# A five-part edit of a fused two-block kernel: transposes a step later, keys copied by DMA, held weights, ordered tables, split low parts

## The chip, the cores and the metric

The kernel runs on one core of a Trainium2 chip. The metric is the device time of one execution in microseconds; the time given for a kernel is the median of its runs. Profiles come from one further execution, recorded by the hardware profiler.

## The reference, cut to what matters

Input x is 512 tokens by 1024 channels, float32. A first block has three sublayers, each with an RMS norm before and after and a residual: a mixer (pooled channels, sparse attention over the best 128 keys, gates), cross attention to 256 memory rows (4 heads of 128), and a SwiGLU feed-forward of width 2816. Then two hybrid layers follow, the part that most of the change touches:

```python
proj = einsum("bld,de->ble", x, w_in)
q, k, v, z_attn, z_ssm, xbc, dt_raw = split(proj)
attn = sliding_window_attention(q, k, v, sinks) * silu(z_attn)   # 16 heads of 64, 4 key heads, window 128
xbc = silu(causal_depthwise_conv(xbc, conv_w, conv_b))
y = ssd_chunked(xs, dt, a, bm, cm) + xs * d_skip
ssm = gated_rmsnorm(y, z_ssm, ssm_norm_w)                        # two groups of 512 channels
x = layer_norm(ALPHA * x + concat(attn, ssm) @ w_out, ln_g, ln_b)
```

## The kernel before, in words

**Tiling.** Channels lie on the 128 partitions and tokens along the free axis, so an activation is eight tiles of 128 x 512, and token halves A and B are columns 0 to 255 and 256 to 511. A projection is made in units of 128 output channels. float32 precision is kept by splitting each operand into a high part in the fast format fp32r and a low part, the remainder: a unit is 24 matmuls (high x high, high x low for eight channel tiles in `mm3`, L147 and L148, then low x high, L152).

**Weights.** `weights` (L100) loads 512 KB into one of three `wraw` tiles by SyncE's queue, ScalarE casts it into one of three `whi` tiles (L107), VectorE writes the remainder into one of three `wlo` tiles (L108). `held` (L111) does the same into tiles of the large pools G or R (34 tiles each), in pieces of 512 columns, so that the three small pools stay free. `units_by_k` (L160) runs four units at once, channel tile by channel tile; the three weights in it that come from `weights` are all in use until its end.

**Order.** Only SyncE's instructions keep the order of the program text. On the other engines a planner at compile time orders instructions by their place in the text, by its own costs and by when it expects operands, and gives out tiles; `issue_after` adds an edge that keeps one instruction behind another on its engine.

**Norms.** `chain`, made by `post_norm` or by a hybrid layer, is a generator: `begin` starts it inside the next layer's first unit, `pump` takes it further by steps, so that the norm of half B runs beside the next layer's units on half A. `inv_sqrt` (L211) needs ScalarE's Ln and Exp, and preloads the table set that has both when a tanh has run since; L224 puts that preload behind the last square.

**The places of the change.** The mixer's first three units (L462 to L472) run by channel tile, with a step of the pending norm after each. The memory layer (L724) takes the output weights of its eight output units from `wo`, of which the first pair is held in G and the others come from `weights`; each of four weight tiles serves two units, first for half A and then for B. The feed-forward (L822) then asks for its first three weights and holds a fourth. A hybrid layer runs gate units, the convolutions and the state-space part, then the keys (L1108; each half of 64 rows is copied to the other 64 partitions by GpSimd at L1114), the values' projection, the second group's norm and the attention loop (L1213). A step of that loop has the scores and the softmax of one head (`scores`: four matmul pairs, VectorE's sum and maximum, ScalarE's Exp, then the scaling by VectorE and GpSimd at L1169), the transposes of the head before (`transposed`: seven, L1183, copied out by ScalarE at L1186), a unit (the next queries or a gate) and, every second step, `values` (L1198) for a pair of heads. GpSimd makes the slopes' table of each head at L1142 in one of nine tiles that the softmax rows share.

Of the kernel before, what the change touches and what calls it, by code (L numbers as in the profile page):

```python
# [14 lines left out]
S = 512  # L15
# [46 lines left out]
class Kern:  # L62
# [37 lines left out]
    def weights(self, src, n=1024):  # L100
# [6 lines left out]
        nc.scalar.copy(hi[:, :n], raw[:, :n])  # L107
        nc.vector.tensor_tensor(lo[:, :n], raw[:, :n], hi[:, :n].bitcast(F32), ALU.subtract)  # L108
        return hi, lo
# [97 lines left out]
    def tanh(self, out, src, scale=1.0):  # L207
        self.ln_set = False
        self.nc.scalar.activation(out, src, AF.Tanh, scale=scale)  # L209

    def inv_sqrt(self, rs, src, u, eps=None, scale=1.0):  # L211
# [7 lines left out]
        if self.ln_set:  # L219
            nc.scalar.activation(rs, src, AF.Ln, **kw)  # L220
        else:
            self.ln_set = True
            with self.tc.issue_after(self.last_sq.ins):
                nc.scalar.preload_act_table_set("natural_log_exp_and_others")  # L224
            with self.tc.issue_after(nc.cur_bb.bb.instructions[-1]):
                nc.scalar.activation(rs, src, AF.Ln, **kw)
# [228 lines left out]
    def mixer(self):  # L455
# [8 lines left out]
        for c in self.HALVES:  # L464
            for k, (x, y) in enumerate(h):
                for pt, m, (whi, wlo) in first:
                    o, cc = pt[:m, c], slice(k * m, k * m + m)
                    nc.tensor.matmul(o, whi[:, cc], x[:, c], start=k == 0, stop=False)
                    nc.tensor.matmul(o, whi[:, cc], y[:, c], start=False, stop=False)
                    nc.tensor.matmul(o, wlo[:, cc], x[:, c], start=False, stop=k == 7)  # L470
                self.pump(1)
            self.pump()  # L472
# [251 lines left out]
    def memory(self):  # L724
# [77 lines left out]
        queries(B, lambda k: values(k // 2, A, pa[k // 2]) if k % 2 else None)  # L802
        wo += [self.weights(a["w_o_mem"][1]), self.weights(a["w_o_mem"][2])]
        for j in range(8):
            if j == 4:
                wo.append(self.weights(a["w_o_mem"][3]))
            out(j, A)
            if j < 4:
                pb.append(logits(j, B))
        for j in range(4):  # L810
            values(j, B, pb[j])
            if j == 0:
                self.head = chain(A)
                self.begin()
        for j in range(8):
            self.pump(1)
            out(j, B)
        self.pump()
        self.head = chain(B)


    def ffn(self):  # L822
# [21 lines left out]
        g = [self.f("ht") for _ in range(2)]  # L844
        first = [self.weights(z) for z in (a["w_gate"][0], a["w_up"][0], a["w_gate"][1])]
        first.append(self.held(a["w_up"][1], "R"))
        for c in self.HALVES:
# [39 lines left out]
    def hybrid(self, L):  # L887
# [220 lines left out]
        for j in range(2):  # L1108
            pt = self.proj(W[j], h)
            ks = [[self.r("G") for _ in range(2)] for _ in range(2)]  # L1110
            for (kh, kl), r, o in zip(ks, (top, bot), (bot, top)):
                self.split(pt[r], kh[r], kl[r], 0.125)
                for t in (kh, kl):
                    nc.gpsimd.tensor_copy(t[o], t[r].bitcast(F32))  # L1114
            kt.append(ks)
# [96 lines left out]
        prs = None  # L1212
        for t in range(17):  # L1213
            j, e_ = divmod(t, 2)
            nxt = scores(t, q) if t < 16 else None
            if t:
                pts[t - 1] = transposed(prs)
            if e_ == 1:
                pz = self.proj(W[32 + j], h)
                g = gate[j] = self.f("R")  # L1220
                self.tanh(g, pz, scale=0.5)
                nc.vector.scalar_tensor_tensor(g, g, 1.0, pz, ALU.add, ALU.mult)
                if j < 7:
                    q = qn
            elif j < 7:
                qn = queries(j + 1)
            if e_ == 0 and t:
                i = j - 1
                pos = values(i, (pts[2 * i], pts[2 * i + 1]))
                nc.vector.tensor_tensor(gate[i], gate[i], pos, ALU.mult)  # L1230
                cat[i] = self.pair(gate[i], "R", 0.5)
            prs = nxt
# [190 lines left out]
```

## Time and profile before

| | |
|---|---|
| median of 3 runs | 1671.53 us (1671.07 to 1672.05) |
| the profiled execution | 1672.5 us, its span 1670.7 us |
| TensorE (PE) busy | 1621.6 us, 97% |
| VectorE (DVE) | 1115.1 us, 67% |
| ScalarE (ACT) | 838.0 us, 50% |
| GpSimd (POOL) | 239.2 us, 14% |
| mean granted TensorE clock | 0.993 |

Times in rows are microseconds from the start of the span unless marked ns; L147 is line 147. In a line of a wait, the instruction on the left waited for the one on the right. In a timeline's line, the figure in brackets is the idle time of the engine before the instruction and what ended it. PEld is TensorE's weight load, which runs beside its matmuls. Roughly, the mixer lies at 39 to 400 us, the memory layer at 380 to 463, the feed-forward at 463 to 820, the hybrid layers at 840 to 1250 and 1255 to 1671; their attention loops are at 1025 to 1154 and 1436 to 1565.

### The profile page before, as it was taken

The numbers are of one execution on the slowest core, as the hardware profiler recorded it, in microseconds if no ns is written. First come the engines' busy times: TensorE is split into PE (matmuls) and PEld (weight loads), VectorE is DVE, ScalarE is ACT, GpSimd is POOL, SyncE is SP. The second block draws the span as 40 slices with busy tenths as digits, with TensorE's granted clock in tenths as the row PEclk, the third lists the DMA queues.
The fourth block names the chain that finished last, engine by engine and source line by source line (L and its number), as shares of the span: only waits on it lengthen the run. The fifth ranks groups of instructions, "written<-read, shape, count | busy, mean of one in ns | idle before, by whom it ended". The sixth has DMA issues, their size and how long they took to land.

```text
span 1670.7 us, 24187 instructions
## 1 busy us (share of the span) xinstructions
PE 1621.6 (97%) x9046; PEld 1362.4 (82%) x9046; DVE 1115.1 (67%) x2199; ACT 838.0 (50%) x1648; POOL 239.2 (14%) x267
## 2 busy tenths in 40 slices
PE   8999999999999999999999999999999999999996
PEld 5778888889888888889988677777998867777786
DVE  6779866548885545523677888765487788866447
ACT  4443255336763233223554776664355477766424
POOL 2010113010200000000000223221230023222121
PEclk9999999999999999999999999999999999999998
DMA  6522322143143233234632122111452211212133
GB/s 223 196 96 76 119 96 76 64 151 119 62 150 104 89 101 101 87 102 129 212 93 89 38 64 89 64 64 56 141 177 82 79 38 57 96 61 65 66 103 112
DMA packets 57719, 166.50 MB, mean 100 GB/s; under 512 B 6673, under 2 KB 15841, under 8 KB 57601
## 3 DMA queue, kind: packets, MB, share of 16 engines
q1 hardware_dynamic: 49216, 155.21, 29.0%
q10 hardware_dynamic: 8384, 9.73, 1.8%
q8 instruction: 71, 1.16, 0.3%
q14 instruction: 48, 0.39, 0.1%
HBM read 158.61 MB, written 8.93 MB: 100 GB/s over the span
## 4 chain that ended last, share of the span: by engine, by line
PE 78%; DVE 11%; ACT 5%; issue 2%; POOL 2%; DMA 1%; SPq 0%; ACTq 0%; DVEq 0%; POOLq 0%
PE psmm L148 21%; PE psmm L152 21%; PE psmm L147 21%; DVE wlo L108 2%; POOL w L1169 2%; PE psmm L175 2%; PE psmm L173 2%; PE psmm L174 2%; ACT w L1164 1%; DVE w L1160 1%; DVE G L130 1%; PE pstr L1061 1%; PE pstr L1183 1%; PE pslg L561 1%; PE pslg L1020 1%
## 5 line engine op out<-in xcount | busy, mean ns | idle before, releaser
L147 PE MATMUL psmm<-G,whi 128*128 128x512 f32 (+1 forms) x1196 | 468.5, 393 | 1.3 <-ACT whi L107 1.3
L148 PE MATMUL psmm<-G,whi 128*128 128x512 f32 (+1 forms) x1196 | 464.3, 389 | 0.0
L108 DVE TENSOR_TENSOR wlo<-wraw,whi 128x1024 fp32r<-128x1024 f32 (+3 forms) x265 | 320.4, 1210 | 184.8 <-ACT whi L107 99.2
L107 ACT CAST whi<-wraw 128x1024 fp32r<-128x1024 f32 (+3 forms) x265 | 270.9, 1025 | 340.3 <-PE psmm L148 291.3
L152 PE MATMUL psmm<-G,wlo 128*128 128x512 f32 (+1 forms) x1196 | 296.3, 388 | 0.0
L148 PEld LDWEIGHTS psmm<-G,whi 128*128 128x128 f32 x1196 | 225.3, 188 | 47.2 <-issue 4.2
L147 PEld LDWEIGHTS psmm<-G,whi 128*128 128x128 f32 x1196 | 225.3, 188 | 47.2 <-issue 2.4
L152 PEld LDWEIGHTS psmm<-G,wlo 128*128 128x128 f32 x1196 | 222.7, 189 | 46.4 <-issue 1.5
L148 PE MATMUL psmm<-R,whi 128*128 128x256 f32 (+1 forms) x732 | 222.7, 326 | 0.0
L147 PE MATMUL psmm<-R,whi 128*128 128x256 f32 (+1 forms) x732 | 222.6, 326 | 0.0
L147 PEld LDWEIGHTS psmm<-R,whi 128*128 128x128 f32 x732 | 139.2, 190 | 11.8 <-issue 0.3
L148 PEld LDWEIGHTS psmm<-R,whi 128*128 128x128 f32 x732 | 139.2, 190 | 11.5
L152 PE MATMUL psmm<-R,wlo 128*128 128x256 f32 (+1 forms) x732 | 138.1, 326 | 0.0
L152 PEld LDWEIGHTS psmm<-R,wlo 128*128 128x128 f32 x732 | 112.8, 190 | 11.5
L198 POOL TENSOR_TENSOR acc<-acc,sq 128x512 f32<-128x512 f32 (+1 forms) x42 | 53.4, 1272 | 454.4 <-ACT sq L197 454.4
L1164 ACT ACTIVATE w<-w,st 128x256 f32<-128x256 f32 (+1 forms) x128 | 60.2, 471 | 33.5 <-DVE st L1162 33.2
L1169 POOL TENSOR_SCALAR w<-w,st 128x256 f32<-128x256 f32 x64 | 46.1, 730 | 134.6 <-DVE st L1167 127.0
L209 ACT ACTIVATE sq<-ht 128x512 f32<-128x512 f32 (+1 forms) x48 | 29.4, 613 | 58.5 <-DVE ht L907 29.3
L1049 POOL TENSOR_TENSOR R<-R,R 128x512 f32<-128x512 f32 x16 | 21.7, 1353 | 228.3 <-ACT R L1048 228.3
L907 DVE SCALAR_TENSOR_TENSOR ht<-psmm,cwh,ht 128x511 f32<-128x511 f32 (+2 forms) x72 | 53.5, 743 | 1.2
L837 DVE TENSOR_TENSOR sq<-psmm,G 128x512 f32<-128x512 f32 (+1 forms) x24 | 15.5, 645 | 57.3 <-PE psmm L152 57.3
L566 POOL TENSOR_TENSOR G<-G,G 128x384 f32<-128x384 f32 (+2 forms) x24 | 28.9, 1217 | 162.1 <-DMA G<-ts 93.4
(348 smaller groups left out, 2701.8 us busy)
## 6 DMA issues: line engine op xcount, KB each, us to landing
wraw<-w_in SPq DMA_DIRECT2D x112, 512.0 KB, 3.4
wraw<-w_out SPq DMA_DIRECT2D x56, 512.0 KB, 3.8
wraw<-w_down SPq DMA_DIRECT2D x24, 512.0 KB, 3.5
wraw<-w_gate SPq DMA_DIRECT2D x22, 512.0 KB, 3.3
wraw<-w_up SPq DMA_DIRECT2D x22, 512.0 KB, 3.3
wraw<-w_down SPq DMA_DIRECT2D x12, 384.0 KB, 3.2
wraw<-w_proj_attn SPq DMA_DIRECT2D x8, 512.0 KB, 3.4
ts<-t SPq DMA_DIRECT2D x4, 640.0 KB, 7.0
```

What stands on the lines that cost most here:

```text
L107: nc.scalar.copy(hi[:, :n], raw[:, :n])
L108: nc.vector.tensor_tensor(lo[:, :n], raw[:, :n], hi[:, :n].bitcast(F32), ALU.subtract)
L147: nc.tensor.matmul(out, whi[:, c], xh, start=start and k == 0, stop=False)
L148: nc.tensor.matmul(out, whi[:, c], xl, start=False, stop=False)
L152: nc.tensor.matmul(out, wlo[:, c], xh, start=False, stop=stop and k == n - 1)
L173: nc.tensor.matmul(o, whi[:, cc], xh[:, c], start=k == 0 and i % 2 == 0, stop=False, skip_group_check=True)
L174: nc.tensor.matmul(o, whi[:, cc], xl[:, c], start=False, stop=False, skip_group_check=True)
L175: nc.tensor.matmul(o, wlo[:, cc], xh[:, c], start=False, stop=k == n - 1, skip_group_check=True)
L198: (eng or nc.gpsimd).tensor_tensor(acc, acc, t, ALU.add)
L907: nc.vector.scalar_tensor_tensor(y[:, s:], pt[:, : S - s], cw(3 - s), y[:, s:], ALU.mult, ALU.add)
L1164: nc.scalar.activation(prs[b], prs[b], AF.Exp, bias=nm[:, b : b + 1], accum_out=sm[:, b : b + 1])
L1169: (nc.gpsimd if b % 2 else nc.vector).tensor_scalar(prs[b], prs[b], rc[:, b : b + 1], 1.0, ALU.mult, ALU.mult)
```

## The change

1. `weights`: the subtraction of the low part is made in pieces of 512 columns.
2. `tanh` keeps its instruction, and `inv_sqrt`'s preload also goes behind the last tanh.
3. The mixer's first units run one after another in each half, with three steps of the pending norm after each.
4. The memory layer holds all four output weights (three in R), and asks for the feed-forward's first three weights during its outputs of half B.
5. The keys' copies to the other 64 partitions are DMAs from ScalarE's queue instead of GpSimd copies.
6. In the attention loop a head's transposes come behind the unit of the following step, and the values one step later; the loop has 18 steps instead of 17. `silu` stands for the two lines that it repeats.

```diff
@@ -105,7 +105,9 @@
         hi = self.wp.tile([P, 1024], F32R, tag="whi", bufs=3, name=self.nm("whi"))
         lo = self.wp.tile([P, 1024], F32R, tag="wlo", bufs=3, name=self.nm("wlo"))
         nc.scalar.copy(hi[:, :n], raw[:, :n])
-        nc.vector.tensor_tensor(lo[:, :n], raw[:, :n], hi[:, :n].bitcast(F32), ALU.subtract)
+        for o in range(0, n, S):
+            c = slice(o, min(o + S, n))
+            nc.vector.tensor_tensor(lo[:, c], raw[:, c], hi[:, c].bitcast(F32), ALU.subtract)
         return hi, lo
 
     def held(self, src, tag, n=1024):
@@ -206,7 +208,7 @@
 
     def tanh(self, out, src, scale=1.0):
         self.ln_set = False
-        self.nc.scalar.activation(out, src, AF.Tanh, scale=scale)
+        self.last_tanh = self.nc.scalar.activation(out, src, AF.Tanh, scale=scale)
 
     def inv_sqrt(self, rs, src, u, eps=None, scale=1.0):
 
@@ -220,7 +222,7 @@
             nc.scalar.activation(rs, src, AF.Ln, **kw)
         else:
             self.ln_set = True
-            with self.tc.issue_after(self.last_sq.ins):
+            with self.tc.issue_after(self.last_sq.ins), self.tc.issue_after(self.last_tanh.ins):
                 nc.scalar.preload_act_table_set("natural_log_exp_and_others")
             with self.tc.issue_after(nc.cur_bb.bb.instructions[-1]):
                 nc.scalar.activation(rs, src, AF.Ln, **kw)
@@ -462,13 +464,9 @@
         first = [(self.ps(), 68, self.weights(a["w_idx"], 8 * 68))]
         first += [(self.ps(), P, self.weights(a["w_in"][next(W)])) for _ in range(2)]
         for c in self.HALVES:
-            for k, (x, y) in enumerate(h):
-                for pt, m, (whi, wlo) in first:
-                    o, cc = pt[:m, c], slice(k * m, k * m + m)
-                    nc.tensor.matmul(o, whi[:, cc], x[:, c], start=k == 0, stop=False)
-                    nc.tensor.matmul(o, whi[:, cc], y[:, c], start=False, stop=False)
-                    nc.tensor.matmul(o, wlo[:, cc], x[:, c], start=False, stop=k == 7)
-                self.pump(1)
+            for pt, m, w in first:
+                self.mm3(pt[:m, c], w, [(x[:, c], y[:, c]) for x, y in h], m)
+                self.pump(3)
             self.pump()
         pt = first[0][0]
         kh, kl = self.r("R"), self.r("R")
@@ -800,10 +798,8 @@
             nc.sync.dma_start(kv[i].bitcast(F32), self.spill[i])
         wo = [self.held(a["w_o_mem"][0], "G")]
         queries(B, lambda k: values(k // 2, A, pa[k // 2]) if k % 2 else None)
-        wo += [self.weights(a["w_o_mem"][1]), self.weights(a["w_o_mem"][2])]
+        wo += [self.held(a["w_o_mem"][j], "R") for j in (1, 2, 3)]
         for j in range(8):
-            if j == 4:
-                wo.append(self.weights(a["w_o_mem"][3]))
             out(j, A)
             if j < 4:
                 pb.append(logits(j, B))
@@ -812,9 +808,12 @@
             if j == 0:
                 self.head = chain(A)
                 self.begin()
+        self.ahead = []
         for j in range(8):
             self.pump(1)
             out(j, B)
+            if j in (1, 3, 5):
+                self.ahead.append(self.weights((a["w_gate"][0], a["w_up"][0], a["w_gate"][1])[j // 2]))
         self.pump()
         self.head = chain(B)
 
@@ -842,8 +841,7 @@
         full = slice(0, S)
         hid += self.pairs("R", 2)
         g = [self.f("ht") for _ in range(2)]
-        first = [self.weights(z) for z in (a["w_gate"][0], a["w_up"][0], a["w_gate"][1])]
-        first.append(self.held(a["w_up"][1], "R"))
+        first = self.ahead + [self.held(a["w_up"][1], "R")]
         for c in self.HALVES:
             for i, pt in enumerate(self.units_by_k(first, h, c)):
                 (up if i % 2 else gate)(i // 2, c, g[i // 2][:, c], pt)
@@ -1111,7 +1109,7 @@
             for (kh, kl), r, o in zip(ks, (top, bot), (bot, top)):
                 self.split(pt[r], kh[r], kl[r], 0.125)
                 for t in (kh, kl):
-                    nc.gpsimd.tensor_copy(t[o], t[r].bitcast(F32))
+                    nc.scalar.dma_start(t[o].bitcast(F32), t[r].bitcast(F32))
             kt.append(ks)
         vs = [self.f("G") for _ in range(2)]
         pv = [self.ps("mm") for _ in range(2)]
@@ -1210,25 +1208,24 @@
         q = queries(0)
         gate, pts = {}, {}
         prs = None
-        for t in range(17):
+        for t in range(18):
             j, e_ = divmod(t, 2)
             nxt = scores(t, q) if t < 16 else None
-            if t:
-                pts[t - 1] = transposed(prs)
-            if e_ == 1:
+            if e_ and t > 2:
+                i = j - 1
+                pos = values(i, (pts.pop(2 * i), pts.pop(2 * i + 1)))
+                nc.vector.tensor_tensor(gate[i], gate[i], pos, ALU.mult)
+                cat[i] = self.pair(gate[i], "R", 0.5)
+            if j < 8 and e_:
                 pz = self.proj(W[32 + j], h)
                 g = gate[j] = self.f("R")
-                self.tanh(g, pz, scale=0.5)
-                nc.vector.scalar_tensor_tensor(g, g, 1.0, pz, ALU.add, ALU.mult)
+                silu(g, pz)
                 if j < 7:
                     q = qn
             elif j < 7:
                 qn = queries(j + 1)
-            if e_ == 0 and t:
-                i = j - 1
-                pos = values(i, (pts[2 * i], pts[2 * i + 1]))
-                nc.vector.tensor_tensor(gate[i], gate[i], pos, ALU.mult)
-                cat[i] = self.pair(gate[i], "R", 0.5)
+            if prs is not None:
+                pts[t - 1] = transposed(prs)
             prs = nxt
 
         order = list(range(8, 16)) + list(range(8))
```

## Rows read from the trace of the kernel before

**Rows 1.** The page: busy times; VectorE's busy tenths in 40 slices.

```profile
PE 1621.6 (97%) x9046; PEld 1362.4 (82%) x9046; DVE 1115.1 (67%) x2199; ACT 838.0 (50%) x1648; POOL 239.2 (14%) x267
...
DVE  6779866548885545523677888765487788866447
```

**Rows 2.** What TensorE waited for: us in total, times, longest us.

```profile
PE pstr L1183 <- POOL w L1169: 5.7, 14, 0.6
PE pslg L1154 <- DVE G L130: 5.0, 2, 2.5
...
PE psmm L147 <- ACT whi L107: 1.3, 1, 1.3
...
PE psmm L470 <- DVE wlo L108: 0.8, 1, 0.8
```

**Rows 3.** Windows of TensorE: busy us (count), mean granted clock, DMA share, GB/s.

```profile
467.00:475.00 8.00, 7.67 (x36) 0.60 0.62 195
479.00:493.20 14.20, 14.20 (x120) 1.00 0.26 89
1025.20:1033.00 7.80, 7.80 (x35) 0.78 0.16 61
1437.00:1441.00 4.00, 4.00 (x16) 0.70 0.10 40
```

**Rows 4.** Groups by line and shape: count | busy us, mean ns | idle before.

```profile
L107 ACT CAST whi<-wraw 128x1024 fp32r<-128x1024 f32 x243 | 254.6, 1050 | 283.5 <-PE psmm L148 248.1 <-PE psmm L174 14.0 <-issue 9.3
...
L1186 ACT COPY ht<-pstr 128x512 f32<-128x512 f32 x32 | 18.7, 585 | 13.6 <-PE pstr L1183 13.3
...
L1186 ACT COPY sq<-pstr 128x384 f32<-128x384 f32 x32 | 15.5, 483 | 4.5 <-PE pstr L1183 4.5
...
L108 DVE TENSOR_TENSOR wlo<-wraw,whi 128x1024 fp32r<-128x1024 f32 x243 | 301.0, 1239 | 159.0 <-ACT whi L107 88.1 <-PE psmm L152 57.2 <-issue 8.2
...
L130 DVE TENSOR_TENSOR G<-psmm,G 64x512 fp32r<-64x512 f32 x32 | 22.0, 688 | 1.3 <-ACT G L129 0.6
...
L108 DVE TENSOR_TENSOR wlo<-wraw,whi 128x512 fp32r<-128x512 f32 x9 | 7.2, 805 | 9.8 <-ACT whi L107 6.5 <-PE psmm L152 3.2
...
L1114 POOL CAST G<-G 64x512 fp32r<-64x512 f32 x16 | 20.3, 1268 | 7.4 <-DVE G L133 5.7 <-PE psmm L1129 0.8 <-issue 0.4
```

**Rows 5.** Timeline of ScalarE and VectorE, first hybrid layer: start us, us, [idle <-releaser].

```profile
984.89 1.28 ACT L209 ACT_TABLE_LOAD   x1
...
1015.08 1.28 ACT L220 ACT_TABLE_LOAD   x1
...
1017.08 1.28 ACT L227 ACT_TABLE_LOAD   x1
...
1019.70 0.69 DVE L230 SCALAR_TENSOR_TENSOR sq<-sq,acc 128x512 f32<-128x512 f32 x1 [2.93 <-ACT sq L229]
```

**Rows 6.** Timeline at the end of the memory layer and the feed-forward's start.

```profile
466.14 2.97 ACT L107 CAST whi<-wraw 128x1024 fp32r<-128x1024 f32 x3
...
466.61 1.19 PE L204 MATMUL pstr<-acc,ones 128*128 128x256 f32 x2 [3.43 <-DVE acc L198]
...
493.20 1.05 ACT L107 CAST whi<-wraw 128x1024 fp32r<-128x1024 f32 x1 [0.57 <-PE psmm L174]
```

**Rows 7.** Timeline at the end of the mixer's first units, VectorE and ScalarE.

```profile
51.77 0.82 DVE L130 TENSOR_TENSOR G<-ht,G 128x256 fp32r<-128x256 f32 x2
...
58.49 0.62 ACT L107 CAST whi<-wraw 128x512 fp32r<-128x512 f32 x1 [6.36 <-PE psmm L469]
```

**Rows 8.** Windows: line 108 alone on VectorE; then all engines, 1220 to 1250.

```profile
380.00:500.00 120.00, 12.12 (x10) 0.97 0.32 104
...
1400.00:1450.00 50.00, 8.58 (x7) 0.97 0.19 64
...
1220.00:1250.00 30.00, 29.48 (x242) 29.03 (x241) 29.93 (x53) 18.46 (x29) 11.11 (x9) 1.00 0.54 170
```

**Rows 9.** DMA issues on ScalarE's queue: count, KB each, median us to landing.

```profile
xd<-G ACTq DMA_DIRECT2D x16, 128.0 KB, 1.7
```

## The prediction

> **What bounds the kernel now.** I read the page's busy shares first, then what TensorE waited for, then the clock by windows, and last the queues around the places that these named. TensorE is busy 97% of the span, VectorE 67%, ScalarE 50% [rows 1]: the reader is to see that only what makes TensorE idle, or slows its clock, can pay much; 49 us of idle are all there is. Four places belong to code that the diff touches. In the list of waits [rows 2]: the attention transposes for the scaled softmax rows (5.7 us in 14 pieces), the first scores of each hybrid layer for the split of the query (5.0 in two pieces), and weights at the start (1.3 and 0.8). In order of time [rows 6]: 3.43 at 466.6, at the end of the memory layer. To these comes the clock: the granted clock is 0.60 on average at 467 to 475, 0.78 at 1025.2 to 1033 and 0.70 at 1437 to 1441 [rows 3], each behind a long idle piece. It switches between 1.2 and 2.4 GHz; these are means of both.
>
> The profiled execution took 1672.5 us around a span of 1670.7; the median of the runs is 1671.5, 1.0 less. I sum against the execution and take the 1.0 off at the end. What a measurement of this kernel can tell from no change is about 0.2%, 3.3 us.
>
> **Attention loop (a head's transposes behind the next unit).** Once in each pair of steps the last two transposes wait 0.4 us for GpSimd's scaling: 14 waits, 5.7 us [rows 2]. In the new order a unit (24 matmuls of 512 columns, over 5 us) stands before them, so the wait goes. What is late next: the copies out of the transposes' banks. Before, a unit stood between transposes and values; now only the next scores do, 8 matmuls, about 1.1 us. The two copies take 0.585 and 0.483, 1.07 together [rows 4]. If ScalarE is free they fit. It was: it sat idle 13.6 us before the first copies, 13.3 of it waiting for the transposes themselves. Behind one weight cast (1.05) the copies end about 0.9 late. GpSimd's slope table for the step after reuses a tile that the transposes free; it comes a unit later too, but only as the following scores run, so it stays covered. Ends: 5.7 gained, to 16 x 0.9 - 5.7 = 8.7 lost. I take 5.7 gained: the idle before the copies is the nearest row.
>
> **Tables in order.** In a hybrid layer the log table's preload was followed at 984.89 by a load back for the last tanh. So the next Ln and the Exp after it loaded again, and the second norm did so once more at 1015.08 and 1017.08 [rows 5]. With the preload behind that tanh, five loads of six become needless per layer (1.28 each), and the first tanh of attention needs one of its own, beside other work. Two of them, 2.57 us, lie in one line: sum, Ln, Exp, VectorE's correction (idle 2.93 before it, [rows 5]), four scalings, and on both queues behind these the first query's split. The first scores waited 2.5 for that split in each layer: 5.0 can go. The clock would not fall: 0.22 x 7.8 = 1.7 in the first layer, 0.30 x 4.0 = 1.2 in the second [rows 3]. That is 7.9 at most. VectorE is busy eight tenths there [rows 1], so a wait may be shortened only in part: I take 6.5, ends 0 and 7.9.
>
> **Memory's output weights held.** Before, three of the four outputs' weights held all whi and wlo tiles until the last output, at 466.6 - 3.4 = 463.2. The casts of the next layer's first three weights ran only at 466.14 to 469.1 [rows 6]; TensorE idled and then ran slowly. With the outputs' weights in R, those casts can run in gaps before, and the feed-forward starts at 463.2 on the first half, which is being finished. Gain by idle and clock: 3.43 + 0.40 x 8 = 6.6. By work: both halves are 192 matmuls at 14.2 / 120 = 0.118 [rows 3], 22.7 us, with three sums of 0.6 it is 24.5 from 463.2, so 487.7 in place of 493.2, where the next cast finds its tile free [rows 6]: 5.5. VectorE must write the second half's activations in that time at eight tenths [rows 1]. SyncE's loads keep their order, the fourth output's only comes earlier. I take 5.0; ends 0 (the twelve R tiles aren't free early, or VectorE is the bound) and 5.5.
>
> **Mixer's first units one after another.** Before, all three weights were in use to the end, so the next cast came at 58.49 [rows 7] and the next unit waited 1.3; the low part cost 0.8 earlier [rows 2]. Now the first weight is free two units (48 matmuls, 5.7) earlier, and the low part is needed only after 16 matmuls: 2.1 gained. Against it: the first unit of the second half wants all eight activation tiles. That half is 72 matmuls, 8.5 us, up to about 59: it would begin near 50, but the last pair of tiles is written until 52.6 [rows 7], and the eight low matmuls follow, to 53.6 rather than 52.8: about 0.8 lost, 1.5 if it begins earlier. Net 0.6 gained; ends 2.1 gained and 1.5 lost.
>
> **Low part split in two.** 243 subtractions of 1024 columns at 1.24 [rows 4] become two each (and twelve of 768). One of 512 is 0.69 for another line that reads PSUM and 0.81 for this line itself [rows 4]: 0.14 to 0.38 more per weight. TensorE sees it only where VectorE is full or waited for; 38 of them lie in four such stretches, of which the first and last stand in [rows 8]: 5 to 14 us of VectorE time, most of it behind TensorE's own work. The first half comes some 0.5 earlier, a gain where the low part is waited for. I take 1.5 lost, ends 1 gained and 14 lost. The Trainium skill speaks against this edit (VectorE: DVE Perf Modes, "Rules for kernel authors": a pipeline flush follows each operation, so keep the count of operations down). By it the upper price holds wherever VectorE bounds; the rows agree that two halves cost more than one whole.
>
> **Keys by ScalarE's queue.** 16 GpSimd copies of 1.27 us [rows 4], 20.3 in all, become 16 transfers of 128 KB. Nearest row: ScalarE's writes of 128 KB land in 1.7 us [rows 9]. The first keys are used only after the values' projection and the first query's unit, the second four heads' from step 8: hidden. VectorE and GpSimd are freer meanwhile; against it, a transfer of a low part stands in ScalarE's queue until VectorE has made it (0.69), and casts stand behind it. I take 0, ends 2 gained and 3 lost.
>
> **Sum.** 5.7 + 6.5 + 5.0 + 0.6 - 1.5 = 16.3 gained: 1672.5 - 16.3 = 1656.2 for a profiled execution, 1655.2 for the median.
>
> **The rivals.**
> *A stage gives nothing.* Memory's gain is eaten by VectorE, or the query's split stays late because VectorE is full: 5.0 to 6.5 less, about 1661. For it: VectorE's eight tenths in both stretches. Against: VectorE's idle of 2.93 while the tables load is just what the change fills.
> *The halves cost.* The doubled subtractions weigh fully in the four stretches: 14 lost in place of 1.5, 1667.7. This is the outcome of counting operations, in rows. Against: at 1220 to 1250 VectorE was busy 29.93 of 30 and TensorE still 29.48 [rows 8].
> *Slower: the values wait for the copies.* The place is the odd step, where values now follow one group of scores after the transposes. If ScalarE has a weight cast (1.05) in front, and also both casts of the query (some 0.6 each) with VectorE's subtraction (0.69) between, the copies end 2.9 + 1.07 behind the transposes, 2.8 late; 16 times it is 45 us, 1700. It decides from 16.3 / 16 = 1.0 us per pair upward. For it: the first of the query's subtractions stands between the two casts in the program. Against: the copies would have to be queued behind instructions that aren't ready.
> *The order is not what the program writes.* Only SyncE keeps the written order; on the other engines a planner may bring the transposes forward again. Then the attention part is 0, 1661.
>
> **How the numbers follow.** Forecast 0.62; one stage missing, or the order undone, 0.20; the halves 0.08; the values' wait 0.10. The forecast's own range is 1648 (nearly all good ends) to 1661. The whole range goes to the halves: 1647 to 1668; what it leaves out is most of the slower rival and little below. Faster: 0.62 + 0.20 + half of the halves' 0.08 = 0.86. Within 0.2%: the other half, and a values' wait of about 1.0, 0.06. Slower: 0.08.
>
> **What would show it.** Right: no wait of the transposes for GpSimd; four table loads fewer per hybrid layer, no 2.5 us before the first scores and the clock at 1.00 after; the feed-forward's casts done before 463, no idle there, its first two halves over near 488. Wrong: values waiting for the copies, the mixer's second half waiting more than 1.5, held weights late for the first output, low parts named as releasers in the tails. A time above 1668, or a gain from stretches that I don't name, would make the prediction wrong.

## The result, and the profile after

The changed kernel took 1654.28 us (median of 4 runs, 1652.12 to 1655.63) beside 1671.79 for the kernel before: ratio 0.9894, 95% interval 0.9878 to 0.9909. In a later job it took 1652.08 beside 1673.73: 0.9873 (0.9858 to 0.9888). The forecast was 1655.2. (The title speaks of five parts; the list of the change has six, and each is run alone below.) The profiled execution took 1655.63, its span 1653.8; a second one, of the later job, 1652.44 and 1650.5.

The page after, busy times and VectorE's tenths, against [rows 1]:

```profile
PE 1616.2 (98%) x9046; PEld 1362.8 (82%) x9046; DVE 1130.3 (68%) x2455; ACT 827.8 (50%) x1643; POOL 208.4 (13%) x251
...
DVE  6779967548886455533767788765597788777447
```

TensorE's idle time (span less busy) fell from 49.1 to 37.6 us, its busy time by 5.4 with the same 9046 matmuls. Part of the 5.4 is clock (its mean went from 0.993 to 0.994); how much isn't settled, since the ends of matmuls are modelled. VectorE has 256 instructions more and 15 us more to do.

What TensorE waited for after, against [rows 2]:

```profile
PE psmm L775 <- ACT ht L131: 2.3, 2, 1.8
PE psmm L149 <- ACT R L131: 2.1, 1, 2.1
PE psmm L177 <- DVE wlo L110: 1.6, 2, 1.1
...
PE psmm L175 <- ACT G L266: 1.3, 1, 1.3
...
PE pstr L1181 <- ACT ht L1184: 0.8, 2, 0.4
...
PE pslg L1152 <- DVE st L1158: 0.7, 2, 0.4
```

The transposes (now L1181) no longer wait for GpSimd, the scores (L1152) no longer for the query's split. Three smaller waits are new or larger, and each gets an experiment below: memory's values for ScalarE (L775), the mixer's pooled part for ScalarE (L149), and a tail for low parts (L177). A fourth, of 1.3 at L175, is the feed-forward's second half waiting for its activations.

The clock behind the three places of [rows 3], and the tables of [rows 5]; windows first (busy us, count, granted clock, DMA share, GB/s), then ScalarE's and VectorE's timeline of the first hybrid layer:

```profile
463.00:471.00 8.00, 7.82 (x64) 1.00 0.34 110
...
1016.80:1024.60 7.80, 7.45 (x39) 1.00 0.01 2
1426.50:1430.50 4.00, 3.66 (x20) 1.00 0.01 2
```

```profile
984.59 1.28 ACT L226 ACT_TABLE_LOAD   x1
1028.67 1.28 ACT L211 ACT_TABLE_LOAD   x1
...
1011.86 0.69 DVE L232 SCALAR_TENSOR_TENSOR sq<-sq,acc 128x512 f32<-128x512 f32 x1 [0.78 <-ACT sq L231]
```

The clock is 1.00 at all three; for the two in the hybrid layers this isn't the edit's doing alone, as the first experiment shows. A hybrid layer has two table loads where it had six, and VectorE's correction waits 0.78 instead of 2.93.

To see where time came from, I compared when the same instruction started or ended in each trace. Lead over the kernel before, in us:

| marker | change | second profile | tables alone | attention alone | memory alone | halves alone |
|---|---|---|---|---|---|---|
| mixer's selection, last sum (L408) | 2.3 | 3.4 | -1.4 | -1.7 | -2.8 | 1.0 |
| mixer's last values (L597) | 1.3 | 4.0 | -1.4 | -1.7 | -2.8 | 2.2 |
| memory's logits, first (L751) | 1.7 | 4.3 | -1.7 | -1.7 | -2.8 | 2.5 |
| memory's last values (L779) | -1.0 | 3.5 | -1.7 | -1.7 | -3.6 | 2.9 |
| hybrid 0 begins (L936) | 3.7 | 8.1 | -1.4 | -1.8 | 1.5 | 3.1 |
| its values' projection ends (L1129) | 5.3 | 9.7 | 0.2 | -1.8 | 1.4 | -0.5 |
| its first attention values (L1198) | 8.5 | 12.9 | 3.3 | -2.4 | 2.1 | -0.3 |
| its tail's first sums (L1263) | 12.1 | 16.5 | 3.3 | 1.4 | 2.3 | 2.6 |
| hybrid 1 begins | 8.5 | 11.8 | 3.3 | 1.4 | 2.3 | -0.9 |
| its first attention values | 13.8 | 17.0 | 8.7 | 1.4 | 3.0 | -2.7 |
| last sums | 16.9 | 20.2 | 8.5 | 4.5 | 2.8 | -0.6 |

What stands before a part's place in its column (-1.4 to -2.8 at the mixer) is a lower clock at 40 to 56 us, or a late first transfer, of that execution; a part is read from one row to the next.

### The profile page after: what moved, and what is told of

The parts are those of the page before. It is cut to its first block, busy times and chain, and to the rows that moved or that the text cites. A ratio compares the mean times of both kernels' runs of the same rounds, so it can differ in the third digit from the quotient of the medians.

```text
span 1653.8 us, 24495 instructions
## 1 busy us (share of the span) xinstructions
PE 1616.2 (98%) x9046; PEld 1362.8 (82%) x9046; DVE 1130.3 (68%) x2455; ACT 827.8 (50%) x1643; POOL 208.4 (13%) x251
## 5 line engine op out<-in xcount | busy, mean ns | idle before, releaser
L149 PE MATMUL psmm<-G,whi 128*128 128x512 f32 (+2 forms) x1244 | 479.5, 388 | 1.2 <-ACT whi L107 1.2
L110 DVE TENSOR_TENSOR wlo<-wraw,whi 128x512 fp32r<-128x512 f32 x515 | 356.5, 712 | 176.0 <-ACT whi L107 144.7
L150 PE MATMUL psmm<-G,whi 128*128 128x512 f32 (+2 forms) x1244 | 474.5, 384 | 0.0
L154 PE MATMUL psmm<-G,wlo 128*128 128x512 f32 (+2 forms) x1244 | 300.8, 382 | 0.0
L149 PEld LDWEIGHTS psmm<-G,whi 128*128 128x128 f32 (+1 forms) x1244 | 233.3, 188 | 49.8 <-issue 5.0
L150 PEld LDWEIGHTS psmm<-G,whi 128*128 128x128 f32 (+1 forms) x1244 | 233.3, 188 | 45.8 <-issue 2.5
L154 PEld LDWEIGHTS psmm<-G,wlo 128*128 128x128 f32 (+1 forms) x1244 | 227.8, 187 | 46.2 <-issue 1.4
L149 PE MATMUL psmm<-R,whi 128*128 128x256 f32 (+1 forms) x684 | 210.4, 329 | 0.0
L150 PE MATMUL psmm<-R,whi 128*128 128x256 f32 (+1 forms) x684 | 210.1, 328 | 0.0
L149 PEld LDWEIGHTS psmm<-R,whi 128*128 128x128 f32 x684 | 130.0, 190 | 11.8 <-issue 0.3
L150 PEld LDWEIGHTS psmm<-R,whi 128*128 128x128 f32 x684 | 130.1, 190 | 11.5
L154 PE MATMUL psmm<-R,wlo 128*128 128x256 f32 (+1 forms) x684 | 130.4, 329 | 0.0
L199 ACT ACTIVATE sq<-G 128x256 f32<-128x256 f32 (+1 forms) x76 | 35.1, 464 | 34.8 <-DVE G L1250 25.9
L1158 DVE CUSTOM_DVE_ANT_0 w<-pslg,w,sinks 128x256 f32<-128x256 f32 (+1 forms) x128 | 51.5, 444 | 1.2 <-issue 0.5
L1047 POOL TENSOR_TENSOR R<-R,R 128x512 f32<-128x512 f32 x16 | 20.6, 1289 | 229.3 <-ACT R L1046 229.3
```

The source lines that it names most:

```text
L110: nc.vector.tensor_tensor(lo[:, c], raw[:, c], hi[:, c].bitcast(F32), ALU.subtract)
L149: nc.tensor.matmul(out, whi[:, c], xh, start=start and k == 0, stop=False)
L150: nc.tensor.matmul(out, whi[:, c], xl, start=False, stop=False)
L154: nc.tensor.matmul(out, wlo[:, c], xh, start=False, stop=stop and k == n - 1)
L199: self.last_sq = nc.scalar.activation(t, src, AF.Square)
L1047: (nc.vector if e_ else nc.gpsimd).tensor_tensor(df, df, cb[hd // 8], ALU.mult)
```

## The experiments

**Each part alone.** e1 takes the second `issue_after`, with `last_tanh`; e2 the 18-step loop; e3 the held output weights and `ahead`; e4 the low parts' pieces:

```diff
-            with self.tc.issue_after(self.last_sq.ins):
+            with self.tc.issue_after(self.last_sq.ins), self.tc.issue_after(self.last_tanh.ins):
```


> The kernel before with part 2 alone (the preload of the log table goes behind the last tanh). In the changed kernel the stretch from the decay to the attention's first values came 5.2 us shorter in each hybrid layer, 10.4 in all, and two parts of the change lie in it: the tables and the keys' DMAs. Theory, the tables do all of it: about 10 faster, near 1661.5, two table loads per layer where there were six, no wait of the first scores above 1 us and a clock of 1.00 behind it. Rival, the tables give what the forecast said (6.5, near 1665.3) and the keys' DMAs, which free GpSimd and VectorE, the other 4. Second rival, VectorE is the bound there: the loads go, and the time stays within 2 of before (1670 or more).

1663.99 beside 1672.65: 0.9947 (0.9933 to 0.9960), 8.7 less. In the trace 4.7 and 5.3 come between the last decay and the first values of the two layers: the first theory, and more than the forecast's 6.5. The kernel before had two more waits in that stretch, which I had left out:

```profile
PE pstr L1061 <- POOL R L1049: 2.1, 2, 1.3
...
PE pstr L204 <- DVE G L1069: 0.7, 2, 0.5
```

Both are where the second norm starts, behind ScalarE's needless loads; both are gone here. By leads, 3.5 of the 10.0 come up to the values' projections (idle 2.1 and 0.7 there), 5.1 from there to the first scores (idle 5.0), and 1.4 between the first scores and the first values, where the clock was 0.78 and 0.70 [rows 3] and is 1.00 here. This last part comes only where the clock falls behind the wait, and it doesn't always. e8 below has all six loads per layer and the same two waits of 2.5, and its clock behind them is 1.00:

```profile
1025.20:1033.00 7.80, 7.40 (x40) 1.00 0.15 59
1436.00:1440.00 4.00, 3.60 (x19) 1.00 0.13 53
```

Six profiles (before, e2, e3, e4, e7, e8) have that wait in both layers; behind five of these twelve waits the clock was lower, behind seven it was 1.00. The kernel before had it low in both layers, and against e8 that cost it 1.2 in all up to the first values. Without that, 8.8 of the 10.0 are left for the tables, beside 8.7 in the times.

```diff
-        for t in range(17):
+        for t in range(18):
...
+            if prs is not None:
+                pts[t - 1] = transposed(prs)
```


> The kernel before with part 6 alone (transposes behind the next unit, values a step later). Theory, the loop's gain is the wait of the transposes for GpSimd and nothing else: from first to last values each loop is 3.1 to 3.5 us shorter, 6.6 in all, near 1665.2, and no wait of the transposes for GpSimd is left. Rival, the loop needs the other parts' slack (the values then wait for the copies out of the transposes' banks): the transposes' wait goes and another of 0.2 us or more per pair comes, 2 gained or less, 1669.5 or more.

1665.98: 0.9960 (0.9948 to 0.9973), 6.7 less. The transposes' waits in this kernel:

```profile
PE pstr L1183 <- POOL w L1169: 0.9, 1, 0.9
...
PE pstr L1183 <- ACT ht L1186: 0.8, 2, 0.4
```

Of 5.7 in 14 pieces [rows 2] one is left; the first theory holds. No values wait for the copies. But ScalarE's idle before the larger copies, 13.6 in [rows 4], is 2.3 in the changed kernel: the cover is thin now.

```diff
+        wo += [self.held(a["w_o_mem"][j], "R") for j in (1, 2, 3)]
...
+                self.ahead.append(self.weights((a["w_gate"][0], a["w_up"][0], a["w_gate"][1])[j // 2]))
```


> The kernel before with part 4 alone (memory's output weights held, the feed-forward's first weights asked for ahead). In the changed kernel the memory layer and the feed-forward's start together gave about 2 us where 5.0 had been forecast: the feed-forward's start gave nearly 5, and the middle of the memory layer lost about 3, with a wait of 1.8 for a tile that ScalarE writes behind three weight casts. Theory, those casts (made for the next layer, drawn forward in front of the activations' casts) take it: also here the middle loses about 3, the whole gains 1 to 3, near 1669.5, and the wait for ScalarE stands there. Rival, the split low parts on VectorE (part 1, not in this kernel) take it: then the whole 5 comes, near 1666.8, and the middle is as before.

1668.72: 0.9977 (0.9969 to 0.9986), 3.9 less. The feed-forward's start gives 5.1 and the middle loses 0.8, not 3: neither theory. So the 2.7 that the middle lost in the changed kernel's first profile needs another cause. ScalarE's timeline there (start, us, what, and in brackets its idle time and what ended it):

```profile
442.48 2.08 ACT L107 CAST whi<-wraw 128x1024 fp32r<-128x1024 f32 x2
...
446.82 1.04 ACT L107 CAST whi<-wraw 128x1024 fp32r<-128x1024 f32 x1
...
450.34 0.62 ACT L131 CAST R<-wraw 128x512 fp32r<-128x512 f32 x1 [1.75 <-DMA wraw<-w_up]
450.86 0.58 ACT L131 CAST ht<-pstr 128x512 fp32r<-128x512 f32 x1
```

and in the second profile of the same kernel:

```profile
445.82 0.62 ACT L131 CAST R<-wraw 128x512 fp32r<-128x512 f32 x1
446.34 0.58 ACT L131 CAST ht<-pstr 128x512 fp32r<-128x512 f32 x1
```

What matters is one instruction in front of another: the cast of the held up weight stands in ScalarE's queue before an activation's cast that the values need. When the weight's transfer lands late, 1.75 us pass for both, and TensorE waits 1.8; in the other execution it had landed, and the middle lost 0.8 as here.

```diff
+        for o in range(0, n, S):
+            c = slice(o, min(o + S, n))
```


> The kernel before with part 1 alone (each low part written in two halves). In the changed kernel the first hybrid layer's tail lost 3.5 us, with three waits of 0.5 to 1.1 for low parts and for ScalarE's casts, and a clock of 0.83 behind them. Theory, the halves take it, since VectorE is full there: slower by 2.5 to 5, near 1675, with waits for low parts between the last attention values and the next layer. Rival, the halves are hidden and it is another part's order that loses it: within 1.5 of before. Second rival, the first half's earlier arrival pays at the starts: 1 faster.

1672.92: 1.0001 (0.9992 to 1.0010). My theory of a slower kernel is false as a total, and right in its place: by the table's last column the first layer's tail loses 3.5. Elsewhere the terms cancel: 2.9 gained up to memory, 2.9 and 2.1 in the attention loops, 3.6 and 3.1 lost from the layers' beginnings to the end of the values' projections, where this kernel waits for low parts:

```profile
PE psmm L1130 <- DVE wlo L110: 5.1, 2, 2.6
PE pslg L1156 <- DVE G L132: 4.9, 2, 2.5
```

That wait is for the second half of a weight. In VectorE's timeline the planner has put five other instructions between its two halves; TensorE goes on at 1007.33, behind the second:

```profile
1001.50 1.10 DVE L110 TENSOR_TENSOR wlo<-wraw,whi 128x512 fp32r<-128x512 f32 x1
...
1006.18 1.10 DVE L110 TENSOR_TENSOR wlo<-wraw,whi 128x512 fp32r<-128x512 f32 x1
```

The gain in attention was a surprise. GpSimd's and VectorE's timelines, first of the kernel before, then with halves:

```profile
1054.79 2.04 POOL L1169 TENSOR_SCALAR w<-w,st 128x256 f32<-128x256 f32 x2 [5.62 <-DVE st L1167]
...
1061.70 0.98 POOL L1169 TENSOR_SCALAR w<-w,st 128x256 f32<-128x256 f32 x2 [4.38 <-DVE st L1167]
...
1055.36 1.21 DVE L108 TENSOR_TENSOR wlo<-wraw,whi 128x1024 fp32r<-128x1024 f32 x1
```

```profile
1054.93 1.50 POOL L1171 TENSOR_SCALAR w<-w,st 128x256 f32<-128x256 f32 x2 [5.47 <-DVE st L1169]
...
1055.50 0.67 DVE L110 TENSOR_TENSOR wlo<-wraw,whi 128x512 fp32r<-128x512 f32 x1
```

Two scalings take 0.98 us undisturbed, 2.04 with a whole low part (1.21) running into them, 1.50 with a half (0.67). This holds for all 64 scalings before: the 15 that overlap a low part take 1.42 us on average, the other 49 take 0.52. So the wait that part 6 hides was made by the low part, and the halves shorten it at its source (two waits, 0.7 in all, are left here): parts 1 and 6 remove the same 5.7, once.

**Parts taken back from the change.** e5 is the change without part 1.

```diff
-        for o in range(0, n, S):
...
+        nc.vector.tensor_tensor(lo[:, :n], raw[:, :n], hi[:, :n].bitcast(F32), ALU.subtract)
```


> The changed kernel with part 1 taken back (low parts in one piece). Alone, the halves moved nothing, by terms that cancel: 2.2 to 2.9 gained up to the memory layer, 2.5 in each attention loop (the transposes' wait for GpSimd, which part 6 removes too), against 4.4 lost at each values' projection and 3.3 in the first hybrid layer's tail. Theory, in the changed kernel only the front's gain and the tail's loss are left of these: without halves the front loses 1 to 2.5 and the tail gives back 3.3, so 1 to 2 faster than the changed kernel, near 1652.5, with no wait for a low part at 1225 to 1250 and the clock at 1.00 there. Rival, the tail's loss comes with the earlier attention end whatever the pieces: then the tail's waits stay and the time is 1 to 2.5 above the changed kernel. Second rival, the attention's gain needs the halves too: 5 above.

1653.15 beside 1672.84: 0.9884 (0.9871 to 0.9898); against the change's 0.9894 and 0.9873 no difference on the chip. In the trace the tail loses nothing, as the theory said: its first sums lead by 12.3, and so does the next layer. All traces agree: the five with halves in that tail (the change twice, e4, e6, e11) lose 3.5 to 4.7 there, the eight without lose nothing. Against the tail's gain stand a larger loss at the mixer's pooled part (3.3 to 0.9 in lead, 2.3 to 1.3 in the change's first profile) and two waits of 0.9 for GpSimd's scaling that whole low parts leave in the attention loops. The same work on all engines as [rows 8], in the change (columns: TensorE, its loads, VectorE, ScalarE, GpSimd), then TensorE's idle there:

```profile
1208.00:1238.00 30.00, 27.88 (x228) 27.25 (x226) 29.83 (x60) 17.18 (x28) 11.49 (x9) 1.00 0.52 161
```

```profile
1235.03 0.38 PE L177 MATMUL psmm<-G,wlo 128*128 128x256 f32 x1 [0.48 <-DVE wlo L110]
...
1237.10 0.38 PE L177 MATMUL psmm<-G,wlo 128*128 128x256 f32 x1 [1.12 <-DVE wlo L110]
1238.11 0.39 PE L175 MATMUL psmm<-G,R 128*128 128x256 f32 x1 [0.62 <-ACT R L131]
```

and without halves:

```profile
1235.87 0.38 PE L175 MATMUL psmm<-G,wlo 128*128 128x256 f32 x1 [0.23 <-DVE wlo L108]
1236.43 0.38 PE L173 MATMUL psmm<-G,R 128*128 128x256 f32 x1 [0.18 <-ACT R L129]
```

VectorE was full before (29.93) and is full after (29.83); there most of what is added comes out at TensorE. (The last of the three waits is for ScalarE's cast of a held weight, which itself waited 2.25 for its transfer.) Line 110 alone on VectorE from 1200 to 1240 in the change, and line 108 in e5:

```profile
1200.00:1240.00 40.00, 19.00 (x25) 0.99 0.54 169
```

```profile
1200.00:1240.00 40.00, 15.45 (x12) 1.00 0.57 175
```

25 halves cost 19.0; 12 wholes cost 15.45, so 12.5 would cost 16.1: 2.9 us more for VectorE. TensorE's idle is 1.8 more, and its clock behind it, 0.83 on average over some 8.2 busy us, costs another 1.4 by estimate; together 3.2 of the 3.6 lost.

```diff
-            if j in (1, 3, 5):
-                self.ahead.append(self.weights((a["w_gate"][0], a["w_up"][0], a["w_gate"][1])[j // 2]))
...
-        first = self.ahead + [self.held(a["w_up"][1], "R")]
+        first = [self.weights(z) for z in (a["w_gate"][0], a["w_up"][0], a["w_gate"][1])]
+        first.append(self.held(a["w_up"][1], "R"))
```


> The changed kernel with the feed-forward's first three weights asked for where they were before (memory's output weights still held). Theory, the casts drawn in front of memory's last softmax rows cost the 2 to 2.6 that the middle of the memory layer lost, and the gain at the feed-forward's start came from the three free cast tiles, not from asking early: the middle is as before the change, the start keeps 3 or more of its 4.7, 1 to 2.5 faster than the changed kernel, near 1652.5. Rival, the start's gain is the early asking itself: it goes, the casts run at the outputs' end again with a wait of 2 to 3.4 and a lower clock, and the time is 2 to 4.5 above the changed kernel. Second rival, held weights' own casts (six of 512 columns, 3.2 together, beside the first outputs) cost the middle: then the middle stays slow without any early casts.

1655.14: 0.9897 (0.9884 to 0.9911), as the change. The two casts run at 441.6 here too, and the wait of 3.4 [rows 6] is gone all the same: held weights free the three cast tiles, and the planner draws the casts forward wherever the text asks for them. The rival of an order undone by the planner thus came true here, at no cost, and not in the attention loop. The rival that credits the early asking falls, and so does my theory of an undisturbed middle: it lost 2.4, and the time isn't lower. Of the 2.4 ScalarE waited 1.1 for the up weight's transfer again.

```diff
-                    nc.gpsimd.tensor_copy(t[o], t[r].bitcast(F32))
+                    nc.scalar.dma_start(t[o].bitcast(F32), t[r].bitcast(F32))
```


> The kernel before with part 5 alone (the keys' copies as DMAs from ScalarE's queue). Theory, the forecast's: hidden, within 1 of before. Rival, freeing GpSimd and VectorE there pays at the first scores, 1 to 2 per layer, 2 to 4 faster. Second rival, the transfers of low parts hold up the casts behind them on ScalarE's queue: 1.5 to 3 slower, with a wait of the values' projection for a cast.

1673.01: 1.0003 (0.9994 to 1.0012). Hidden, as forecast; the 16 transfers land in 2.3 us.

```diff
+            for pt, m, w in first:
+                self.mm3(pt[:m, c], w, [(x[:, c], y[:, c]) for x, y in h], m)
+                self.pump(3)
```


> The kernel before with part 3 alone (the mixer's first units one after another). In the changed kernel the sparse selection's first sums came 1.6 earlier and its last 2.3, in the kernel with halves alone 0.4 and 1.0. Theory, parts add: here about 1.2 gained at that place, near 1671.4. Rival, the second half's first unit waits for the last activation tile (the forecast's 0.8 to 1.5 lost): no gain at that place or a loss of up to 1.5.

1670.71: 0.9986 (0.9977 to 0.9995), 2.1 less. The selection's last sum leads by 2.6; the second half's unit does not wait for the last activation tile. By the mixer's values 2.3 of it is given back in this profile, and hybrid 0 begins level with the kernel before. The 1.6 by which this profile ends ahead come in the hybrid layers, 1.2 of them behind the two waits whose clock was told of above; the part doesn't touch them. So the time's 2.1 isn't shown to be the mixer's. TensorE at the pooled part, and two windows:

```profile
98.66 0.50 PE L147 MATMUL psmm<-R,R 128*128 128x512 f32 x1 [2.63 <-ACT R L129]
```

```profile
95.00:100.00 5.00, 2.37 (x9) 0.93 0.84 260
100.00:105.00 5.00, 5.00 (x18) 0.73 0.07 26
```

That wait was 1.4 before: the casts that it waits for begin 1.3 earlier (97.99, not 99.33), TensorE comes 2.6 earlier. VectorE's shifted sums stand between. Behind the longer idle the clock is lower, but not in every execution, as the next runs show.

**Four kernels in one job.** e9 is the change itself, e10 has the halves in the mixer alone:

```diff
+        self.piece = 1024
...
+        for o in range(0, n, self.piece):
```


> The changed kernel itself, run beside the three that follow, so that they are compared on one chip: 1654 to 1655.5, 0.989 of before. If it stands 1 us or more above the kernel with halves in the mixer alone, the halves behind the mixer cost.

> The changed kernel with low parts in halves only up to the mixer's end, whole from the memory layer on. Without any halves the front reached the mixer's last values 1.0 ahead of before, with them 2.2 ahead, and the first hybrid layer's tail lost nothing without them and 3.3 to 3.5 with them. Theory, both are local: the mixer's 1.2 stays, the tail loses nothing, 2 to 4 faster than the changed kernel of the same job, near 1651.8. Rival, the mixer's 1.2 is given back by the feed-forward's start (which was level at 4.4 to 5.0 in both): as without halves, 1653. Second rival, the tail depends on where the attention ends and not on the pieces: no gain over the changed kernel.

(`piece` is 512 until the memory layer sets it.) The change: 1652.08, 0.9873 (0.9858 to 0.9888). Halves in the mixer alone: 1651.55, 0.9866 (0.9850 to 0.9882). The intervals overlap, so no faster version is shown, and both expectations were missed: the change came 2 below its 1654 to 1655.5, and e10 only 0.5 below the change, not 2 to 4. The traces agree with both local claims: with halves in the mixer alone the tail loses nothing (13.2 and 13.3 in lead), while the change lost 4.7 there (16.5 to 11.8). But the change's profile kept the mixer's gain this time, which a slow clock had cost it in the first one. The window 95 to 105 in its first profile, and in its second:

```profile
95.00:105.00 10.00, 7.90 (x28) 0.83 0.46 153
```

```profile
95.00:105.00 10.00, 7.90 (x35) 1.00 0.31 110
```

The same work behind the same idle of 2.1 us, but another granted clock, so that 35 instead of 28 matmuls fit; the lead at the mixer's last values is 1.3 with the one and 4.0 with the other (1.1 of this by an earlier first transfer). All eight profiles with part 3 idle 2.1 to 2.6 us there: six go on at 0.83, two (this one and e12) at 1.00.

```diff
-                    nc.scalar.dma_start(t[o].bitcast(F32), t[r].bitcast(F32))
+                    nc.gpsimd.tensor_copy(t[o], t[r].bitcast(F32))
```


> The changed kernel with part 5 taken back (the keys copied by GpSimd again). Halves alone brought a wait of 2.6 for a low part into each values' projection, with the keys' copies on GpSimd beside it, 4.4 lost there per layer; in the changed kernel that wait isn't there. The keys' DMAs alone moved nothing. Theory, the DMAs are what removes that wait: here it comes back, 4 to 9 slower than the changed kernel, 1659 to 1663. Rival, the tables' order (ScalarE earlier) removes it: no wait, within 1 of the changed kernel.

1652.89: 0.9878 (0.9864 to 0.9893), as the change, with no wait at the values' projection. My theory falls: the DMAs aren't what removes it. The tables' order is the only other part at work in that stretch. In this trace the second half of the low part runs 4.8 us behind the projection's first matmul, in e4 7.9, so VectorE stands earlier against TensorE; that the tables' order alone does this was not isolated.

```diff
-        wo += [self.held(a["w_o_mem"][j], "R") for j in (1, 2, 3)]
+        wo.append(self.held(a["w_o_mem"][1], "R"))
...
+            if j in (1, 3):
+                wo.append(self.held(a["w_o_mem"][j // 2 + 2], "R"))
```


> The kernel with halves in the mixer alone, and memory's held weights asked for one by one (the third and fourth during the outputs of half A) in place of all three before them. In the changed kernel six casts of 512 columns (3.2 us) stand in one piece on ScalarE ahead of those outputs, and the middle of the memory layer lost 2.4 to 2.7 whether or not the next layer's weights were asked for early. Theory, that burst costs the middle: here it loses 1 or less, 1 to 2 faster than the kernel with halves in the mixer alone, and the feed-forward's start keeps its gain. Rival, the middle loses because TensorE reaches the norm's sum and the softmax rows sooner (waits of 1.5 for the sum and 0.6 for the row scale stay): no difference, within 0.7.

1652.59: 0.9875 (0.9860 to 0.9890). No gain over e10: my theory falls. The logits lose 0.2 instead of 1.2, but TensorE then waits 2.8 instead of 1.5 for the norm's sum. That is the rival's mechanism: what stands last there is the norm. The 1.0 between the two times lies outside the rival's 0.7, but the intervals overlap.

## Why the prediction was right, step by step

The total came out because no term had a large error, and partly by luck: memory's came out below its forecast where the others came out above. Measured alone, the parts sum to 8.7 + 6.7 + 3.9 + 2.1 - 0.3 - 0.2 = 20.9, beside 17.5 and 21.7 for the change in its two jobs. That this sum fits is luck too: it holds the 5.0 that the halves gain in the attention loops, which part 6 gains already, and the 6.7 that they lose up to the end of the values' projections, which the change doesn't lose. The change's two profiles end 3.3 apart: 1.1 by a first transfer that lands later, 1.6 by the mixer's clock and 1.8 by the up weight's landing, less 1.1 that the second lost more in the tail. So the forecast's 16.3 was low by a few us where these delays don't fall.

- *Attention, 5.7:* 6.7 (4.5 to 8.7) alone. The step holds: the wait goes and values don't wait for copies, so the slower rival is out. I read GpSimd as the cause; the low part beside it was.
- *Tables, 6.5:* 8.7 (6.7 to 11.2) alone. Right mechanism, undersized: I followed the loads to the first scores only and left out the 2.8 that they cost at the second norm's start. The clock, 2.9 of my upper end, was oversized: between first scores and first values the traces give 1.4, and a wait of that length is followed by a lower clock only in some executions. That VectorE would let only a part through was wrong.
- *Memory, 5.0:* 3.9 (2.3 to 5.2) alone. The start gave 5.1, by the tiles that become free. A wait of 1.34 for the second half's activations is new there, as its bound said. What I missed is the queue in front of the values: a held weight's cast, with its transfer, costs 0.8 to 2.7 in the middle.
- *Mixer, 0.6:* 2.1 (0.8 to 3.8) alone, of which the trace shows 2.6 at the selection and 0.3 at the mixer's end. The feared wait of the second half does not show; the price is a later one, at the pooled part, and its size hangs on the clock of the execution.
- *Halves, -1.5:* -0.3 (-1.7 to 1.3) alone, but not for the reason given. The rival that counts operations is right in one place: a tail where VectorE is full lost 3.6 and 4.7 in the change's two profiles. In the kernel before, the attention loops gained 5.0 by halves, and no step of mine had that; in the change part 6 has it already, and the halves keep a gain in the mixer and at two scalings. My price per weight, 0.14 to 0.38, was too high for most of the kernel: halves alone give VectorE 20.6 us more for 256 weights, 0.08 each, and 0.23 each in the full tail. My row for the tail [rows 8] showed TensorE at 29.48 beside a full VectorE, and I took that for slack; it was the last of it. Low parts as releasers in that tail, one of my signs of being wrong, did come.
- *Keys, 0:* within measurement, as forecast.

Open: why the granted clock and the landing of the up weight differ between executions of one kernel; and which part removes the wait at the values' projection.

## What to carry to other kernels

An engine that is full for 30 us has no slack, even if the one behind it still runs: an edit that adds work there is priced at up to its full busy time, plus the clock behind the idle. Cutting an instruction in two also lets the planner put other work between the pieces. Before a lower clock is put down to a wait, compare other executions with the same wait. Follow a needless table load to every consumer of ScalarE's and VectorE's queues behind it, not only to the longest wait. When a wait names GpSimd, look at what VectorE ran beside it before moving the waiter.

## What the runs showed of the hardware that I had not expected

GpSimd's scaling of 128 x 256 is held up while VectorE subtracts two tiles: a pair takes 0.98 alone, 2.04 beside a subtraction of 1.21 and 1.50 beside one of 0.67, so the excess (1.06, 0.52) goes with the length of VectorE's instruction, and both delayed pairs end 0.26 behind that instruction's end. The Trainium skill (SBUF — State Buffer, "SBUF: two separate sides") says that a VectorE operation with two SBUF inputs and a GpSimd operation that reads SBUF exclude each other for a whole instruction; the traces agree. It works the other way too: in e4 VectorE's subtraction of 512 columns takes 1.10 beside GpSimd's copies of keys (1001.50 and 1006.18 above) and 0.67 at 1055.50. So splitting the same work helped a neighbour (mean of 64 scalings 730 ns before, 642 with halves), though it cost VectorE itself 2.9 us in 40.

The granted clock behind one and the same idle differs between executions of one kernel: 0.83 and 1.00 over 95 to 105 us in the change's two profiles, behind 2.1 us of idle. Behind the 3.43 of [rows 6] it was low in all six profiles that have this wait.
